# Two token tiles of values and gates placed ahead of the second half's recurrent units in a two-layer streaming encoder

## The chip, the cores and the metric

The program runs on one core of one Trainium2 chip. The metric is device microseconds of one execution. TensorE (PE) multiplies matrices into PSUM banks, VectorE (DVE) and ScalarE (ACT) do elementwise work and empty PSUM, GpSimd (POOL) does elementwise work on on-chip memory, and SyncE's queue (SP) issues most transfers.

## What is computed

One inference step for 576 tokens (64 sample tokens, then 512 prompt tokens) through two layers. Each layer is an FFN, a mixer and a second FFN, each between RMS norms. The mixer projects the normed input h once; the columns of that projection feed three head groups:

```python
h = _rmsnorm(x, ng[2])
z = h @ p['w_in'][l]
q_a, kv_a, kpe_raw, hq, hf, hi, hg, cu, cv = jnp.split(z, offsets, axis=-1)
o_a, c_new, kpe_new = _mla(q_a, kv_a, kpe_raw, pos, ...)
o_b, S_new = _hgrn2(hq, hf, hi, hg, lb_all[l], p['hgrn_out_g'][l], ...)
o_c, v_new = _chunk_mlp(cu, cv, p['cmlp_v_g'][l], p['cmlp_w_s'][l], p['cmlp_b_s'][l])
mix = jnp.concatenate([o_a, o_b, o_c], axis=-1) @ p['w_out'][l]
x = x + _rmsnorm(mix, ng[3])
```

The recurrent group (`_hgrn2`) takes queries hq and forget gates hf (4 x 128 columns in all), the values hi and the output gates hg (256 columns each), and scans over the tokens:

```python
S_new = exp(b_last)[..., None] * S + einsum('bshe,bshd->bhed', kc * exp(b_last[:, None] - b), vc)
o = _rmsnorm(o_inter + o_intra, out_g) * silu(hg)
```

## The kernel before

All matmuls of the projections are in split precision: a float32 operand is kept as a high part and a low part (tiles `hh`, `hl` of h; `wh`, `wl` of the weights), and a product is three matmuls (`three`, L144; `nat3`, L590). A weight chunk of 128x1024 (`chunk`, L118; `cols`, L131) is one transfer into `wr`, one ACT copy to `wh` (L126) and one DVE subtraction to `wl` (L127). The pool of `wr` has 6 buffers, those of `wh` and `wl` 7 each.

The 576 tokens are handled with features on the partitions in two halves of 288 columns (`HALF`). For tiles with tokens on the partitions there are five starts (`tcol`): columns 0, 64, 192, 320 and 448. A tile reads 128 columns from its start, so tiles 0 and 1 end at column 192, within the first half, and tile 2 reaches into the second.

The end of the FFN hands over half by half. For each half the generator `post` (L243) scales the eight feature tiles `d`, adds them into `x` and calls `pre` (L186), which makes `hh`, `hl` and the sum of squares (on POOL, L198). `pre_stats` (L200) then makes the factor of the norm: column sums on PE (`ss`, L68), a power on POOL (L151), a transposing spread on PE (`bc`, L73) and a copy to `rbc` on ACT (L215). The generators are stepped by an estimate of PE's time (`tick`, `until`). At the end of `units` for half 0, `zout(z, o, 0)` steps them until the first half's factor is there, and by their due times the whole `post` of the second half has then been issued.

In `mixer` (L1041) the four recurrent units `chs` (hq and hf, 128 columns each, chunks loaded ahead by the FFN) are multiplied for half 0 and then for half 1 (`units`, `together`, 8 k times 4 units times 3 matmuls, tile `u`). Each unit and half takes a PSUM bank of the tag "mm", which has 6. `zout` (L1035) evacuates the four banks of a half to `z` on DVE and scales them with `rbc`. Then `nat_chunks` asks for the four chunks `nch` of the 512 columns of values and gates (two k each), and `natural` (L597) multiplies them tile by tile (24 matmuls of 128x512 into one bank, tile `n`); ACT evacuates to `vg` with the factor `r` (L1066). After the first of the five, z of half 1 is evacuated and the generator `hgrn` (L645) is spawned. It makes `lf` and `k` (ACT, two table loads), a scan, and then 14 levels of DVE, ACT, POOL and PE work (`zb` L706, `lv`, `at` L721), beside which the main loop goes on with five tiles `uv` and five tiles of latents. It waits for all five `vg` only after the levels.

The order written out is a priority. The tile scheduler orders each engine's instructions by it and by when they are ready in its own estimate, and gives out buffers and banks as they come free; on the chip each engine then keeps that order. A buffer comes free with the last instruction that uses it.

Of the kernel before, what the change touches and what calls it, by code (L numbers as in the profile page):

```python
# [11 lines left out]
AF = mybir.ActivationFunctionType  # L12
# [24 lines left out]
RC = (0, 1, 3, 4, 5)  # L37
# [12 lines left out]
class Net:  # L50
# [990 lines left out]
    def mixer(self, l, gpost, gpre, nxt, packed):  # L1041
        nc, tin = self.nc, self.i
        w = tin["w_in"][l]
        r, r2 = self.rn, self.rn2
        c, a = {}, {"q": [], "qr": [], "kt": {}, "ktc": {}, "v": [], "vc": [], "oT": {}}
        self.mixh, self.mixl = {}, {}
        chs = self.ahead
        z = [self.slot("z") for _ in range(4)]
        for hf in (0, 1):
            o = self.units(chs, hf)  # L1050
            if hf == 0:
                self.zout(z, o, 0)
        self.stow()
        vg = {}
        self.left, self.attn_left, self.gated, self.decayed = 10, 20, False, False

        c["og"] = self.gain_rows("hgrn_out_g", l)
        nch = self.nat_chunks(w, 1216, 512)
        for i in range(5):
            ps = self.natural(nch, i, 512)  # L1060
            if i == 0:
                self.zout(z, o, 1)
                self.spawn(self.hgrn(l, z[2:], z[:2], vg))
                z = o = None
            t = self.slot("vg")
            nc.scalar.activation(t[:, :512], ps, AF.Copy, scale=r[:, RC[i]:RC[i] + 1])  # L1066
            vg[i] = t

        self.spawn(self.spatial(l, c))
        uv = []  # L1070
# [1 line left out]
        nch = self.nat_chunks(w, 1728, 512)  # L1072
        for i in range(5):
            ps = self.natural(nch, i, 512)
            t = self.slot("uv")
# [7 lines left out]
        nch = self.nat_chunks(w, 384, 320)  # L1083
# [3 lines left out]
        for i in range(5):  # L1087
            ps = self.natural(nch, i, 320)
# [6 lines left out]
        for u in range(3):  # L1095
            ps = self.unit(self.cols(w, u * P))
# [26 lines left out]
        def query(u):  # L1123
            ps = [self.mm("q"), self.mm("q")]
            for k in range(3):
                for (c0, n), pp in zip(HALF, ps):
                    self.three(pp[:, :n], wqh[k][:, u], wql[k][:, u], qah[k][:, c0:c0 + n], qal[k][:, c0:c0 + n], k == 0, k == 2)
                self.tick()
            return ps
# [47 lines left out]
        for h in range(HEADS):  # L1177
            ps = query(h)
# [8 lines left out]
            for c0, n in HALF:  # L1187
                ps = self.mm("k")
# [4 lines left out]
            ps = self.mm("k")  # L1193
# [14 lines left out]
        for k0 in (4, 0):  # L1208
# [5 lines left out]
            chs = {}  # L1214
# [242 lines left out]
```

## Time and profile before

| | |
|---|---|
| median of 3 runs | 2313.14 us (2313.03 to 2313.42) |
| the profiled execution | 2313.43 us |
| its span, first to last instruction | 2311.6 us |
| mean granted TensorE clock | 0.979 |
| PE busy | 2217.3 us (96%) |
| DVE busy | 1594.7 us (69%) |
| ACT busy | 1114.0 us (48%) |
| POOL busy | 225.4 us (10%) |

Busy shares are over the whole span; a stage can have another limit. PE's matmuls are pipelined and a shown duration overlaps the next; the spacing of starts gives the rate. Times in the views are microseconds from the span's start. Layer 0's change of stage is at about 412 to 465 us, layer 1's 1143.2 us later.

### The profile page before, as it was taken

The numbers are of one execution on the slowest core, as the hardware profiler recorded it, in microseconds if no ns is written. First come the engines' busy times: TensorE is split into PE (matmuls) and PEld (weight loads), VectorE is DVE, ScalarE is ACT, GpSimd is POOL, SyncE is SP. The second block draws the span as 40 slices with busy tenths as digits, with TensorE's granted clock in tenths as the row PEclk, the third lists the DMA queues.
The fourth block names the chain that finished last, engine by engine and source line by source line (L and its number), as shares of the span: only waits on it lengthen the run. The fifth ranks groups of instructions, "written<-read, shape, count | busy, mean of one in ns | idle before, by whom it ended". The sixth has DMA issues, their size and how long they took to land.

```text
span 2311.6 us, 39493 instructions
## 1 busy us (share of the span) xinstructions
PE 2217.3 (96%) x15892; PEld 2155.0 (93%) x15892; DVE 1594.7 (69%) x2671; ACT 1114.0 (48%) x1945; POOL 225.4 (10%) x230
## 2 busy tenths in 40 slices
PE   8999999998899899999989999999988998999998
PEld 7999999888799799999979999998887998999998
DVE  6888643787567888744588885438875678877443
ACT  7444442465554644443355444325646546444423
POOL 0000000343301100000020000004332020000000
PEclk9999999999999899999999999999999999999999
DMA  6333442222122233344123334423121312333421
GB/s 195 103 101 92 119 133 83 92 57 77 60 59 65 90 101 96 88 128 132 47 86 101 93 90 122 132 74 101 39 86 48 96 60 83 93 92 103 118 77 42
DMA packets 339787, 211.06 MB, mean 91 GB/s; under 512 B 17634, under 2 KB 319956, under 8 KB 339604
## 3 DMA queue, kind: packets, MB, share of 16 engines
q1 hardware_dynamic: 339604, 208.54, 30.3%
q8 instruction: 125, 2.05, 0.4%
q14 instruction: 58, 0.48, 0.1%
HBM read 190.11 MB, written 18.38 MB: 90 GB/s over the span
## 4 chain that ended last, share of the span: by engine, by line
PE 76%; DVE 14%; ACT 4%; issue 3%; POOL 3%; DMA 0%; SPq 0%; POOLq 0%; DVEq 0%; ACTq 0%
PE d L68 23%; PE X L68 22%; PE Q L68 11%; PE R L68 6%; PE wo L68 4%; PE u L68 3%; DVE zb L706 2%; PE n L68 2%; DVE hl L142 2%; DVE x L256 1%; PE sc L68 1%; DVE d L253 1%; DVE wl L127 1%; DVE wl L139 1%; PE q L68 1%
## 5 line engine op out<-in xcount | busy, mean ns | idle before, releaser
L68 PE MATMUL d<-gh,wh 128*128 128x288 f32 x1408 | 413.5, 297 | 2.7 <-ACT gh L138 2.7
L68 PE MATMUL d<-gl,wh 128*128 128x288 f32 x1408 | 413.9, 295 | 0.0
L68 PE MATMUL d<-gh,wl 128*128 128x288 f32 x1408 | 412.7, 294 | 0.0
L127 DVE TENSOR_TENSOR wl<-wr,wh 128x1024 fp32r<-128x1024 f32 (+2 forms) x174 | 203.4, 1173 | 175.9 <-ACT wh L126 175.1
L126 ACT ACTIVATE wh<-wr 128x1024 fp32r<-128x1024 f32 (+2 forms) x174 | 174.8, 1008 | 287.3 <-PE d L68 163.9
L68 PE MATMUL X<-th,wh 128*128 128x288 f32 x960 | 286.8, 299 | 0.0
L68 PE MATMUL X<-tl,wh 128*128 128x288 f32 x960 | 285.5, 297 | 0.0
L68 PE MATMUL X<-th,wl 128*128 128x288 f32 x960 | 284.5, 296 | 0.0
L68 PEld LDWEIGHTS d<-gh,wh 128*128 128x128 f32 x1408 | 262.3, 187 | 3.6 <-ACT gh L138 3.6
L68 PEld LDWEIGHTS d<-gh,wl 128*128 128x128 f32 x1408 | 264.8, 188 | 0.0
L68 PEld LDWEIGHTS d<-gl,wh 128*128 128x128 f32 x1408 | 264.1, 188 | 0.0
L138 ACT ACTIVATE wh<-wr 128x1024 fp32r<-128x1024 f32 x160 | 168.4, 1055 | 148.0 <-PE R L68 68.5
L139 DVE TENSOR_TENSOR wl<-ws,wh 128x1024 fp32r<-128x1024 f32 x120 | 147.0, 1225 | 105.4 <-ACT wh L138 105.2
L139 DVE TENSOR_TENSOR wl<-wr,wh 128x1024 fp32r<-128x1024 f32 x160 | 194.7, 1222 | 8.2 <-ACT wh L138 6.8
L138 ACT ACTIVATE wh<-ws 128x1024 fp32r<-128x1024 f32 x120 | 127.3, 1060 | 150.4 <-DVE ws L497 97.8
L151 POOL TENSOR_TENSOR p<-m,mhalf 128x3 f32<-128x3 f32 (+1 forms) x14 | 14.4, 1028 | 1739.4 <-DVE m L234 1535.1
L68 PEld LDWEIGHTS X<-th,wl 128*128 128x128 f32 x960 | 183.1, 191 | 0.0
L68 PEld LDWEIGHTS X<-tl,wh 128*128 128x128 f32 x960 | 182.8, 190 | 0.0
L68 PEld LDWEIGHTS X<-th,wh 128*128 128x128 f32 x960 | 182.6, 190 | 0.0
L390 DVE TENSOR_TENSOR d<-d,d 128x288 f32<-128x288 f32 x128 | 55.2, 454 | 179.6 <-PE d L68 179.5
L68 PE MATMUL u<-hh,wh 128*128 128x288 f32 x480 | 148.3, 312 | 3.0 <-ACT x L1363 1.5
L68 PE MATMUL u<-hl,wh 128*128 128x288 f32 x480 | 148.0, 309 | 1.2 <-DVE hl L142 1.2
(364 smaller groups left out, 5857.6 us busy)
## 6 DMA issues: line engine op xcount, KB each, us to landing
wr<-ffn_w_gate SPq DMA_DIRECT2D x160, 256.0 KB, 3.0
wr<-ffn_w_up SPq DMA_DIRECT2D x160, 256.0 KB, 3.4
wr<-ffn_w_down SPq DMA_DIRECT2D x64, 512.0 KB, 4.2
wr<-w_in SPq DMA_DIRECT2D x30, 512.0 KB, 3.7
xd<-x SPq DMA_DIRECT2D x48, 288.0 KB, 2.1
x<-xd SPq DMA_DIRECT2D x48, 288.0 KB, 6.0
wr<-ffn_w_down SPq DMA_DIRECT2D x32, 384.0 KB, 3.6
wr<-w_out SPq DMA_DIRECT2D x16, 512.0 KB, 3.4
```

The costliest lines, as they stand in the source:

```text
L68: self.nc.tensor.matmul(out, lhsT, rhs, start=start, stop=stop, skip_group_check=onto)
L126: nc.scalar.activation(hi[:, :a * b], raw[:, :a * b], AF.Copy)
L127: nc.vector.tensor_tensor(lo[:, :a * b], raw[:, :a * b], hi[:, :a * b].bitcast(F32), op=ALU.subtract)
L138: nc.scalar.activation(hi, src, AF.Copy)
L139: nc.vector.tensor_tensor(lo, src, hi.bitcast(F32), op=ALU.subtract)
L142: nc.vector.scalar_tensor_tensor(lo, src, scale, hi.bitcast(F32), op0=ALU.mult, op1=ALU.subtract)
L151: self.nc.gpsimd.tensor_tensor(out, m, self.mhalf[:, :n], op=ALU.pow)
L253: nc.vector.scalar_tensor_tensor(d[s][:, sl], d[s][:, sl], gpost[s], bc, op0=ALU.mult, op1=ALU.mult)
L256: nc.vector.tensor_tensor(self.x[k][:, sl], self.x[k][:, sl], d[k][:, sl], op=ALU.add)
L390: nc.vector.tensor_tensor(d[m][:, sl], d[m][:, sl], ps[hf][:, :n], op=ALU.add)
L706: nc.vector.tensor_tensor(zo, qv[rs, :, h:], ev[rs, :, h:], op=ALU.mult)
```

## The change

In `mixer` the loop over the halves is opened up. Between `zout(z, o, 0)` and the units of half 1, the chunks `nch` are asked for and `natural` runs for tiles 0 and 1, each with its ACT evacuation to `vg`. Then come the units of half 1, the stores of `x` (`stow`), the gains, `zout(z, o, 1)` directly, the spawn of `hgrn`, and tiles 2 to 4. The set of instructions is the same.

```diff
-        for hf in (0, 1):
-            o = self.units(chs, hf)
-            if hf == 0:
-                self.zout(z, o, 0)
+        vg = {}
+
+        def rows(nch, i):
+            t = self.slot("vg")
+            nc.scalar.activation(t[:, :512], self.natural(nch, i, 512), AF.Copy, scale=r[:, RC[i]:RC[i] + 1])
+            vg[i] = t
+
+        o = self.units(chs, 0)
+        self.zout(z, o, 0)
+
+        nch = self.nat_chunks(w, 1216, 512)
+        for i in range(2):
+            rows(nch, i)
+        o = self.units(chs, 1)
         self.stow()
-        vg = {}
         self.left, self.attn_left, self.gated, self.decayed = 10, 20, False, False
-
         c["og"] = self.gain_rows("hgrn_out_g", l)
-        nch = self.nat_chunks(w, 1216, 512)
-        for i in range(5):
-            ps = self.natural(nch, i, 512)
-            if i == 0:
-                self.zout(z, o, 1)
-                self.spawn(self.hgrn(l, z[2:], z[:2], vg))
-                z = o = None
-            t = self.slot("vg")
-            nc.scalar.activation(t[:, :512], ps, AF.Copy, scale=r[:, RC[i]:RC[i] + 1])
-            vg[i] = t
+        self.zout(z, o, 1)
+        self.spawn(self.hgrn(l, z[2:], z[:2], vg))
+        z = o = None
+        for i in range(2, 5):
+            rows(nch, i)
```

## Rows read from the trace of the kernel before

**Rows 1.** The page: busy us, share and count; then the chain's shares.

```profile
PE 2217.3 (96%) x15892; PEld 2155.0 (93%) x15892; DVE 1594.7 (69%) x2671; ACT 1114.0 (48%) x1945; POOL 225.4 (10%) x230
...
PE 76%; DVE 14%; ACT 4%; issue 3%; POOL 3%; DMA 0%; SPq 0%; POOLq 0%; DVEq 0%; ACTq 0%
```

**Rows 2.** The chain in order of time: start, duration, what, matmuls.

```profile
64.94 3.20 PE Q L68 x24
...
448.15 9.62 PE u L68 x60
...
458.79 14.77 PE n L68 x65
```

**Rows 3.** Windows: stretch, length, busy us (instructions) per engine, clock, DMA.

```profile
436.00:448.00 12.00, 7.99 (x59) 7.45 (x59) 11.45 (x23) 4.62 (x12) 6.92 (x7) 1.00 0.48 171
1579.20:1591.20 12.00, 9.42 (x59) 8.83 (x58) 11.45 (x23) 4.62 (x12) 6.95 (x7) 0.86 0.49 169
448.00:464.00 16.00, 16.00 (x92) 14.89 (x92) 7.71 (x12) 4.62 (x6) 4.03 (x10) 0.89 0.45 130
464.00:474.00 10.00, 10.00 (x50) 8.36 (x48) 6.57 (x8) 7.14 (x10) 3.77 (x3) 1.00 0.20 56
530.00:546.00 16.00, 11.52 (x75) 10.75 (x76) 15.01 (x25) 10.26 (x15) 4.86 (x4) 0.95 0.38 118
613.00:630.00 17.00, 14.38 (x56) 11.90 (x57) 7.04 (x21) 12.81 (x30) 1.83 (x3) 0.71 0.05 10
```

**Rows 4.** Timeline of PE: start, duration, instruction, idle before it and releaser.

```profile
442.19 0.63 PE L73 MATMUL bc<-ident_c,rn 64*128 64x64 f32 x3 [2.05 <-POOL rn L151]
...
447.32 0.83 PE L68 MATMUL ss<-ones,acc 128*128 128x1 f32 x6 [1.96 <-POOL acc L198]
...
449.05 0.44 PE L68 MATMUL u<-hh,wh 128*128 128x288 f32 x1
449.29 0.44 PE L68 MATMUL u<-hl,wh 128*128 128x288 f32 x1
...
457.61 0.39 PE L68 MATMUL n<-wh,hh 128*128 128x512 f32 x1
...
545.10 0.69 PE L73 MATMUL tp<-ident_c,cn 128*128 128x128 f32 x2 [4.48 <-DVE cn L897]
```

**Rows 5.** Timeline of DVE, layer 0: the splits of weights, z, the first lf.

```profile
429.75 1.21 DVE L127 TENSOR_TENSOR wl<-wr,wh 128x1024 fp32r<-128x1024 f32 x1
...
444.44 1.21 DVE L127 TENSOR_TENSOR wl<-wr,wh 128x1024 fp32r<-128x1024 f32 x1
...
446.54 1.54 DVE L1039 TENSOR_TENSOR z<-u,rbc 128x288 f32<-128x288 f32 x4
...
448.26 1.22 DVE L127 TENSOR_TENSOR wl<-wr,wh 128x1024 fp32r<-128x1024 f32 x1
...
457.97 2.36 DVE L127 TENSOR_TENSOR wl<-wr,wh 128x1024 fp32r<-128x1024 f32 x2 [5.89 <-ACT wh L126]
460.25 1.54 DVE L1039 TENSOR_TENSOR z<-u,rbc 128x288 f32<-128x288 f32 x4
...
467.43 1.22 DVE L668 TENSOR_SCALAR lf<-lf 128x576 f32<-128x576 f32 x1 [4.50 <-ACT lf L663]
```

**Rows 6.** Timeline of ACT, layer 0: a late chunk, then the start of hgrn.

```profile
449.77 1.06 ACT L126 ACTIVATE wh<-wr 128x1024 fp32r<-128x1024 f32 x1 [4.48 <-PE u L68]
...
463.69 0.69 ACT L1066 ACTIVATE vg<-n,rn 128x512 f32<-128x512 f32 x1 [3.56 <-PE n L68]
...
464.84 1.28 ACT L661 ACT_TABLE_LOAD   x1
466.14 0.69 ACT L661 ACTIVATE k<-z 128x576 f32<-128x576 f32 x1
```

**Rows 7.** Timeline of DVE, layer 1: chunk 1 of nch and z.

```profile
1587.64 1.21 DVE L127 TENSOR_TENSOR wl<-wr,wh 128x1024 fp32r<-128x1024 f32 x1
1589.76 1.54 DVE L1039 TENSOR_TENSOR z<-u,rbc 128x288 f32<-128x288 f32 x4
```

## The prediction

> **What bounds the kernel now.** I read the page first: TensorE (PE) is busy 96% of the span and carries 76% of the chain that ended last [rows 1], so mostly what counts is PE time. But the change touches one place per layer, so I went on to the windows there. From 436 to 448 us in layer 0, and from 1579.2 to 1591.2 us in layer 1, VectorE (DVE) is busy 11.45 of 12 us and PE only 7.99 and 9.42 [rows 3]. The reader is to see a stretch that PE doesn't bound: the norm of the second token half (`post`, `pre`) runs on DVE, ScalarE (ACT) and GpSimd (POOL) while PE has the recurrent units to do. Then the PE timeline for what ends PE's waits: 2.05 us for the factor of the first half (POOL, then `bc`), 1.96 us for POOL's sum of squares (`ss`) [rows 4]. That is 4.0 us per layer, the most that filler work could win there. Then the DVE and ACT timelines, for when the filler could start and what depends on its place [rows 5, 6], and the windows up to the end of the level loop of `hgrn`. From 530 to 546 us DVE is at 15.01 of 16 us, and PE stalls again, 4.48 us, for a DVE result [rows 3, 4]. So behind this place it is DVE, with `hgrn`'s chain, that sets the pace at least as much as PE.
>
> **What moves.** No instruction is added or removed. Per layer 48 matmuls of 128x512 (`natural` 0 and 1, 8 k times 3 each) and two ACT evacuations go ahead of the second half's 96 matmuls, and the 4 chunks of `nch` are now asked for before `units(chs, 1)`. A moved n matmul takes 14.77/65 = 0.227 us [rows 2]. A u matmul is 128x288, like the Q matmuls, which take 3.20/24 = 0.133 us [rows 2]. So 48 x 0.227 = 10.9 us of PE work per layer change place. Three resources decide when it really runs.
>
> *PSUM.* The tag "mm" has 6 banks. `units(chs, 0)` holds 4 until `zout(z, o, 0)`, which DVE does at 446.54 us [rows 5]. In the kernel before, the other two go to the first two units of half 1: of their 96 matmuls about 36 are done before the `ss` at 447.3 us, and 60 follow it [rows 2]. In the kernel after, natural 0 and 1 come earlier in the program and take these two banks, so none of the 96 can start before about 447 us. The filler displaces 36 x 0.133 = 4.8 us of work that already fills this hole.
>
> The Trainium skill ("Perfetto Trace Analysis", Identifying Performance Opportunities) says that a gap on the engine that should be busy can mean too little PSUM for the next tile. The trace is in line with it: 60 of the 96 run only after the evacuations of z have freed banks.
>
> *The weights of the filler.* A natural tile needs chunk 0 for k 0 and 1, chunk 1 for k 2 and 3, and so on. DVE finishes the low part of chunk 0 at 430.96 us, of chunk 1 at 445.65, of chunk 2 at 449.48 [rows 5]. Everything of `post` for both halves stands ahead of these splits in the program both before and after, so I leave these times where they are. Before 448 us, then, the filler has k 0 to 3 of two tiles: 24 x 0.227 = 5.4 us, against the 4.8 us displaced. That is 0.6 us won, not 4.0.
>
> *The seventh buffer.* The pool of high parts has 7 buffers; the recurrent chunks hold 4. So chunk 3 of `nch` is only split when the units let one go: ACT takes it at 449.77 us, after waiting 4.48 us for PE's u [rows 6]. In the kernel after, all four units end together, so chunk 3 and the chunks of the second `nch` come only then, and k 6 and 7 of both tiles (12 matmuls, 2.7 us) fall behind the units.
>
> **The sum, layer 0.** PE's u matmuls ahead of `ss` end at 447.32 - 1.96 = 445.4 us; the 36 of half 1 among them and the wait and `bc` (2.05 + 0.4, since the next start follows 0.4 us on) take 7.3, so the first half's units end at about 438. PE after: 12 n to 440.7, nothing until chunk 1 at 445.65, 12 n to 448.4, `ss` to 449.0, then 96 u and the 12 n of chunk 2: 12.8 + 2.7 = 15.5, to 464.5 us. Before, the units ended at 457.6 [rows 4], and at 464.5 PE had done (464.5 - 458.0)/0.227 = 29 of the n matmuls; after, it has done 36. PE would be 7 x 0.227 = 1.6 us ahead.
>
> Against that the clock: behind the two waits of before, u matmuls start 0.24 us apart instead of 0.133 [rows 4]; the mean granted clock from 448 to 464 us is 0.89 [rows 3], so part of it ran at the lower of the two levels (1.2 GHz, of 2.4). Some 13 matmuls are hit, 1.4 us lost. The new order leaves PE idle for 1.5 + 2.9 us with 0.6 us of `bc` between, so I expect the same fall, perhaps longer, meeting n matmuls also: between 0 and 3 us more lost than before. PE is then 1.6 us ahead to 1.4 us behind, so even.
>
> `hgrn` pays. Its z of half 1 was evacuated at 460.25 [rows 5], and moves to 464.5, or to 466.5 with the clock low: 4.2 to 6.2 us later. Some of that was slack: before, ACT held the first sigmoid until 466.14, because the evacuation of natural 0 (463.69) and a table load (464.84, 1.28) stood ahead [rows 6]. After, natural 0 ends later than the z, so the sigmoid only has chunk 3's split (1.06, the same instruction as at 449.77) and the table load ahead: 464.5 + 1.06 + 1.28 = 466.8 to 468.8, so 0.7 to 2.7 us late. On DVE, chunk 3's low part and two of the second `nch` (2.36 us at 457.97) were done before z; now they lie behind it. DVE then idles 4.50 us ahead of its first `lf` [rows 5], which hides one of them (1.2 us); the other two, 2.4 us, fall among instructions of a stretch in which DVE has 3.4 of 10 us free [rows 3]. Between 0 and 2.4 us; I take 1.3, as the free time is mostly waits inside the chain. Sum: 0.7 to 5.1 us late per layer, with 3.0 the middle (1.7 + 1.3). If that cover in the idle 4.50 us is gone, 1.2 more.
>
> Passed on to the end? The chain runs through `hgrn`'s DVE and ACT steps to 545 us, where PE waits 4.48 us for DVE [rows 4], so I pass it whole. Layer 1 has the same order (chunk 1 at 1587.64, z at 1589.76, as 444.44 and 446.54 moved by 1143.2) [rows 5, 7]; its clock fell earlier, in the window that shows 0.86 [rows 3]. Two layers: 2 x 3.0 = 6.0. The profiled execution took 2313.43 (span 2311.6), 0.3 above the median 2313.14; the forecast is 2313.1 + 6 = 2319, its own range 2314.5 (2 x 0.7) to 2323.3 (2 x 5.1).
>
> **Rivals.** *It washes out* (0.30). For: PE comes out even; the stretch from 613 to 630 us has PE busy 14.38 of 17 at a mean clock of 0.71 [rows 3], so a late `hgrn` may meet a wait that is there anyway; the sigmoid may move ahead of natural 0's evacuation and give back up to 4.3 us (466.14 less 461.79, the end of z). Also here: the tile scheduler, which orders by readiness, leaves the two banks with the units, and the change does nothing. Time 2311 to 2316, likeliest 2313.4.
>
> *It does what such an order is for* (0.20). If DVE splits chunks 1 and 2 before the last steps of `post`, 36 n matmuls (8.2 us) are ready, the 4.0 us of waits are filled, and the units still start at 447 us, so the 36 u displaced come back as 36 n that needn't run later: 4.0 us per layer, 2313.1 - 8 = 2305. Against: DVE has only 0.55 us free in that window [rows 3], and two splits are 2.4 us. It decides for this case if chunk 1's low part ends before about 441 us.
>
> By the Trainium skill ("Perfetto Trace Analysis", Optimization Strategy) interleaving regimes that load different engines can help; that speaks for this rival, and the DVE windows against it.
>
> *Worse than forecast* (within the forecast's chance): `ss` stands ahead of the second 12 n in PE's order, so these wait until 448 us, and the clock falls for longer: 2.5 us more per layer, 2324.
>
> **How the numbers follow.** Forecast 0.50, washed out 0.30, faster 0.20; the worse order is within the 0.50. About 0.2%, 4.6 us, is what a measurement here can tell from no change. The forecast case spans that bound (2 x 0.7 = 1.4 us at its low end), so I put 0.13 of its 0.50 under it, and 0.02 of the washed-out 0.30 above it. So faster 0.20, same 0.13 + 0.28 = 0.41, slower 0.37 + 0.02 = 0.39. The range for 8 in 10 runs from the faster rival's time, 2305, to the high end of forecast and worse order together, 2 x (5.1 + 2.5) = 15.2 above the median: 2328.
>
> **What would show it.** Right: between 438 and 447 us PE shows n matmuls and no u of half 1, with waits of over 2 us; 96 u after `zout`; z of half 1 evacuated at 464 to 467; the third and fourth n of each tile's chunks behind 445. Wrong: u of half 1 ahead of 446 us (the banks stayed); chunk 1's low part on DVE well before 444; first sigmoid at or before 466; the levels (`zb`, L706) ending where they did, though z is late, which would say that PE and not `hgrn` sets the end.

## The result and the profile after

| | before | after |
|---|---|---|
| median | 2313.09 us | 2336.83 us (2334.19 to 2339.29, 4 runs) |
| ratio to before, 95% interval | | 1.0104 [1.0087, 1.0122] |
| profiled execution, its span | 2313.43, 2311.6 us | 2335.09, 2333.3 us |

The kernel became slower by 23.7 us, or 12.0 us per layer by the ratio. The forecast was 2319 (2305 to 2328): the sign was right, and the time lies beyond the range.

The page of the kernel after (busy us, share, count; then the chain's shares), which answers to [rows 1]:

```profile
PE 2228.8 (96%) x15892; PEld 2160.4 (93%) x15892; DVE 1589.0 (68%) x2671; ACT 1113.9 (48%) x1945; POOL 225.0 (10%) x230
...
PE 77%; DVE 13%; ACT 3%; issue 3%; POOL 3%; DMA 0%; SPq 0%; POOLq 0%; DVEq 0%; ACTq 0%
```

The counts are the same, and no share moves by more than a point. The page alone would show nothing; the windows do. After (stretch, length, busy us with instructions of PE, PEld, DVE, ACT, POOL, clock, DMA share, GB/s), at the places of the first three of [rows 3], set to the later start of the stage (in layer 0 the first u starts at 422.37 us, where before has 421.50):

```profile
437.00:449.00 12.00, 6.41 (x34) 5.05 (x33) 11.45 (x23) 4.57 (x11) 6.93 (x7) 0.89 0.47 169
449.00:465.00 16.00, 16.00 (x91) 14.64 (x92) 1.32 (x3) 0.41 (x1) 0.86 (x1) 0.87 0.15 46
1590.60:1602.60 12.00, 7.54 (x34) 5.75 (x34) 11.45 (x24) 4.57 (x11) 6.92 (x7) 0.75 0.47 165
```

In the hole (the 12 us around PE's two waits) of layer 0 PE does 6.41 us of work where it did 7.99, in layer 1 7.54 for 9.42. In the 16 us behind it DVE has 1.32 us to do where it had 7.71, and ACT 0.41 for 4.62: the two engines that carry `hgrn`'s chain stand still while PE does the units. The timeline of PE, after (start, duration, instruction, idle before it and releaser), for [rows 4]:

```profile
438.45 0.30 PE L68 MATMUL u<-hh,wl 128*128 128x288 f32 x1
438.58 0.39 PE L68 MATMUL n<-wh,hh 128*128 128x512 f32 x1
...
443.06 0.63 PE L73 MATMUL bc<-ident_c,rn 64*128 64x64 f32 x3 [2.03 <-POOL rn L151]
443.45 0.48 PE L68 MATMUL n<-wh,hh 128*128 128x512 f32 x1
...
448.20 1.44 PE L68 MATMUL ss<-ones,acc 128*128 128x1 f32 x6 [3.57 <-POOL acc L198]
449.50 0.77 PE L68 MATMUL n<-wl,hh 128*128 128x512 f32 x1
...
450.92 0.63 PE L68 MATMUL n<-wl,hh 128*128 128x512 f32 x1
451.35 0.63 PE L68 MATMUL n<-wh,hl 128*128 128x512 f32 x1
...
454.03 0.30 PE L68 MATMUL u<-hh,wh 128*128 128x288 f32 x1
...
469.98 0.30 PE L68 MATMUL u<-hh,wl 128*128 128x288 f32 x1
```

Ten n stand ahead of `bc` and four ahead of `ss`; no u of the second half runs before 454.03. The wait for POOL's `acc` grew from 1.96 to 3.57 us, and the n behind it start 0.43 us apart instead of 0.227. DVE, after, for [rows 5]:

```profile
445.32 1.21 DVE L127 TENSOR_TENSOR wl<-wr,wh 128x1024 fp32r<-128x1024 f32 x1
...
447.42 1.54 DVE L1039 TENSOR_TENSOR z<-u,rbc 128x288 f32<-128x288 f32 x4
...
468.50 1.19 DVE L1039 TENSOR_TENSOR z<-u,rbc 128x288 f32<-128x288 f32 x3 [17.21 <-PE u L68]
469.61 1.22 DVE L127 TENSOR_TENSOR wl<-wr,wh 128x1024 fp32r<-128x1024 f32 x1
470.74 0.45 DVE L1039 TENSOR_TENSOR z<-u,rbc 128x288 f32<-128x288 f32 x1
471.11 3.49 DVE L127 TENSOR_TENSOR wl<-wr,wh 128x1024 fp32r<-128x1024 f32 x3
477.49 0.96 DVE L668 TENSOR_SCALAR lf<-lf 128x576 f32<-128x576 f32 x1 [2.89 <-ACT lf L663]
```

DVE idles 17.21 us for the units. The last z starts at 470.74; before, the one group of four began at 460.25. ACT, after, for [rows 6]:

```profile
468.30 3.90 ACT L126 ACTIVATE wh<-wr 128x1024 fp32r<-128x1024 f32 x4 [7.85 <-PE u L68]
472.66 0.69 ACT L1053 ACTIVATE vg<-n,rn 128x512 f32<-128x512 f32 x1 [0.46 <-PE n L68]
473.38 0.42 ACT L881 ACTIVATE vg<-vg 128x256 f32<-128x256 f32 x1
473.74 0.69 ACT L1053 ACTIVATE vg<-n,rn 128x512 f32<-128x512 f32 x1
474.46 0.42 ACT L881 ACTIVATE vg<-vg 128x256 f32<-128x256 f32 x1
474.90 1.28 ACT L661 ACT_TABLE_LOAD   x1
476.19 0.69 ACT L661 ACTIVATE k<-z 128x576 f32<-128x576 f32 x1
```

From the moment the units let buffers go, four chunk copies, two evacuations with their gates and a table load, 7.9 us, stand in ACT's queue ahead of the first sigmoid. It comes at 476.19 instead of 466.14.

The next views are of DVE's waits inside the 14 levels (engine, line, what it waited for: us in total, times, longest). Before, from 476.8 us:

```profile
DVE zb L706 <- ACT e L698: 5.8, 6, 1.3
```

After, from 488.7 us:

```profile
DVE zb L706 <- ACT e L698: 6.3, 4, 2.1
DVE at L721 <- PE lv L68: 4.9, 4, 1.9
DVE rk L895 <- POOL rk L151: 1.3, 2, 0.7
```

A wait is new: DVE comes to the masked copy `at` before PE has made its `lv`, four times, 4.9 us. The levels take 70.8 us from first to last `zb`, where they took 62.6.

### The profile page after: what moved, and what is told of

The parts are those of the page before. It is cut to its first block, busy times and chain, and to the rows that moved or that the text cites. A ratio compares the mean times of both kernels' runs of the same rounds, so it can differ in the third digit from the quotient of the medians.

```text
span 2333.3 us, 39500 instructions
## 1 busy us (share of the span) xinstructions
PE 2228.8 (96%) x15892; PEld 2160.4 (93%) x15892; DVE 1589.0 (68%) x2671; ACT 1113.9 (48%) x1945; POOL 225.0 (10%) x230
## 4 chain that ended last, share of the span: by engine, by line
PE 77%; DVE 13%; ACT 3%; issue 3%; POOL 3%; DMA 0%; SPq 0%; POOLq 0%; DVEq 0%; ACTq 0%
PE d L68 23%; PE X L68 22%; PE Q L68 10%; PE R L68 5%; PE wo L68 4%; PE n L68 3%; PE u L68 3%; DVE hl L142 2%; DVE zb L706 1%; DVE x L256 1%; PE sc L68 1%; DVE d L253 1%; DVE wl L127 1%; DVE wl L139 1%; POOL gr L151 1%
```

## The experiments

All times below count from the first u of the layer, which removes what earlier stages shift. "z" is the start of the last z of the second half, "k" the first sigmoid, "levels" the length from first to last `zb`, "lv" the last matmul of the levels, "n" the last `n<-wh,hh` (the last k) of the five-tile streams, "wo" the first matmul of the projection that ends the mixer; layer 0, in us. "Per layer" is the ratio less one, times 2313.1, over two.

| kernel | us | ratio, 95% | per layer | z | k | levels | lv | n | wo |
|---|---|---|---|---|---|---|---|---|---|
| before | 2313.1 | | | 39.8 | 44.6 | 62.6 | 129.6 | 138.5 | 239.4 |
| after | 2336.8 | 1.0104 [1.0087, 1.0122] | +12.0 | 48.4 | 53.8 | 70.8 | 141.6 | 145.2 | 251.4 |
| one tile ahead | 2321.7 | 1.0039 [1.0024, 1.0054] | +4.5 | 40.7 | 45.1 | 68.2 | 132.0 | 140.9 | 246.4 |
| none ahead | 2314.2 | 1.0007 [0.9997, 1.0016] | +0.8 | 38.3 | 38.4 | 64.9 | 118.3 | 138.0 | 240.0 |
| evacuations late | 2334.1 | 1.0093 [1.0078, 1.0108] | +10.8 | 48.4 | 48.4 | 73.8 | 136.8 | 141.0 | 247.2 |
| two units first | 2319.8 | 1.0033 [1.0021, 1.0046] | +3.8 | 45.4 | 41.4 | 73.0 | 132.4 | 136.0 | 242.9 |
| z and spawn late | 2324.0 | 1.0045 [1.0029, 1.0061] | +5.2 | 38.3 | 48.5 | 71.3 | 135.0 | 138.6 | 243.0 |
| k 0, 1 ahead | 2328.9 | 1.0066 [1.0049, 1.0082] | +7.6 | 46.6 | 47.7 | 67.1 | 128.2 | 147.3 | 249.8 |
| denser hgrn | 2345.3 | 1.0139 [1.0124, 1.0154] | +16.1 | 48.8 | 54.2 | 67.8 | 136.0 | 151.2 | 256.7 |
| forget first | 2302.3 | 0.9953 [0.9938, 0.9968] | -5.4 | 34.5 | 33.1 | 63.1 | 113.6 | 131.8 | 233.5 |
| banks held | 2332.1 | 1.0079 [1.0063, 1.0096] | +9.1 | 46.7 | 51.9 | 62.6 | 135.6 | 144.6 | 245.4 |
| banks held, later | 2328.1 | 1.0068 [1.0053, 1.0083] | +7.9 | 45.2 | 50.4 | 62.6 | 134.8 | 143.7 | 246.1 |
| spawn late | 2318.9 | 1.0028 [1.0017, 1.0039] | +3.2 | 38.0 | 48.1 | 70.4 | 133.7 | 137.3 | 242.8 |

### How much comes with the number of tiles

One tile ahead (against after: one tile in the first loop, four in the second), and none (no tile ahead, but `nch` early, and z and the spawn ahead of all five):

```diff
-        for i in range(2):
+        for i in range(1):
             rows(nch, i)
...
-        for i in range(2, 5):
+        for i in range(1, 5):
```

> Only tile 0 runs ahead of the second half's units, tile 1 goes back behind them. Theory A (late z): matmuls of the tiles that stand between the two z evacuations delay z of half 1 and with it hgrn, and each us of it reaches the end. One tile holds one bank and puts 18 to 24 n matmuls (4.1 to 5.4 us) ahead of z, so about half the loss: 2322 to 2326. Theory B (idle PE and low clock in the gap are the loss): the gap is as empty as with two tiles, so the loss stays mostly: 2330 to 2336. Theory C (the earlier request of the chunks and the new place of zout and hgrn are the loss): 2333 to 2337.

> No tile runs ahead; the chunks are still asked for before the second half's units, and zout and the spawn of hgrn still stand before all five tiles. Theory A: z of half 1 is back at its old time, and the first sigmoid no longer stands behind the evacuation of tile 0 (463.69 to 466.14 in the kernel before), so the time is that of before or up to 4.3 us per layer less: 2305 to 2313. Theory B: 2313. Theory C: the loss stays, 2330 to 2337.

One tile costs 4.5 us per layer, two cost 12.0, none 0.8, with an interval that includes zero. The first time is 0.3 us under theory A's range, the second about 1 us above A's and B's. So the early `nch` and the direct `zout` are not the cause. The kernel with none says more: its sigmoid is 6.2 us earlier than before, its last `lv` 11.2 and its last `zb` 2.0 us earlier, yet n and wo stay. An earlier `hgrn` alone brings nothing here: the stream of tiles on PE ends when it did.

### The late sigmoid

Against after, the evacuations of tiles 0 and 1 are written behind `hgrn`'s first step:

```diff
...
-        for i in range(2):
-            rows(nch, i)
+        held = [self.natural(nch, i, 512) for i in range(2)]
...
         self.spawn(self.hgrn(l, z[2:], z[:2], vg))
+        self.step(self.bg[-1])
+        for i in range(2):
+            put(i, held[i])
```

> The changed kernel, but the ACT evacuations of tiles 0 and 1 are written after hgrn's first step, so that ACT's order has the sigmoids ahead of them. Theory A: the sigmoid starts about 5 us earlier than in the changed kernel (it stood at 476.2 with both z ready at 471.2); if each us reaches the end, 2 x 5 less: 2326 to 2328. Theory B or C: the start of hgrn isn't the loss, 2334 to 2338.

The sigmoid came 5.4 us earlier, as the edit wants, and the time fell by 2.7 us in all, which the spread of the runs doesn't tell from nothing (the two intervals overlap); 9 to 11 were expected. So the queue on ACT in front of the sigmoid, the most striking rows of after, is not what most of the 23.7 us hang on.

### The banks

Against after, two of the four units of the second half are put ahead of the two tiles, so that they get the two free banks, and the other two behind:

```diff
+        o = self.units(chs[:2], 1)
         for i in range(2):
             rows(nch, i)
-        o = self.units(chs, 1)
+        o += self.units(chs[2:], 1)
```

> Two of the four units of half 1 first, then tiles 0 and 1, then the other two units; everything else as changed. The two free banks go to units again and PE's gap is filled as before the change. Theory A: 36 to 48 n matmuls (8 to 11 us) still stand ahead of the last z, so most of the loss stays: 2327 to 2334. A variant of B (the banks: PE's hole left empty is the loss): 2313 to 2318.

All 48 n still run ahead of the last u, but the hole is filled by u, as this window shows against [rows 3]:

```profile
439.50:451.50 12.00, 9.94 (x63) 9.62 (x62) 11.45 (x22) 5.13 (x12) 6.26 (x7) 0.86 0.43 148
```

PE has 9.94 us of work there, and the cost falls from 12.0 to 3.8 us per layer; the time lies between the two ranges written down, nearer to the banks'. This points to the two banks and not to the work put ahead of the units. It doesn't settle it, since the forget units are evacuated early here too and the sigmoid comes 12.4 us earlier than in after; the kernels with the banks held do. Next, the reverse: the tiles take the banks, but only the 12 n whose weights are ready (k 0 and 1 of both tiles) are written ahead.

```diff
...
-        for i in range(2):
-            rows(nch, i)
+        begun = [self.natural(nch, i, 512, None, range(2)) for i in range(2)]
...
+        for i in range(2):
+            rows(nch, i, begun[i], range(2, KT))
```

> Both tiles take their banks ahead of the units, but only k 0 and 1 (12 matmuls) are written ahead; the other 36 come behind z and hgrn's first step. The banks are taken and PE's gap is as empty as in the changed kernel; what is gone is the work between the two z evacuations. If the hole alone costs (2.4 to 4.5 us per layer by the traces): 2318 to 2322. If the banks and the hole were the whole loss of 12 us per layer: 2333 to 2337. If only the displaced work cost: 2311 to 2315.

With 18 n ahead of the last u, where after has 38, 7.6 us per layer remain; the time, 2328.9, is in none of the ranges written down, and nearest to that of the whole loss. Last, the order of before, with the two banks held by empty tiles until z of the first half is out. The first version (held from before the first half's units) also took banks from those, which then needed 20.5 us from first to last start instead of 16.1; the second asks for the banks only behind them. Each adds two memsets and two copies of one column per layer. In the second these don't delay the hole: `bc` and `ss` start 20.7 and 25.5 us after the first u, in before 20.7 and 25.8.

```diff
             if hf == 0:
+                hold = [self.mm("hold") for _ in range(2)]
+                for t in hold:
+                    nc.vector.memset(t[:, 0:1], 0.0)
                 self.zout(z, o, 0)
+                for t in hold:
+                    nc.vector.tensor_copy(t[:, 0:1], z[3][:, 0:1])
+                hold = None
```

> The kernel before in its own order, with the two free banks held by an empty tile each until z of half 0 is evacuated (four instructions of one column on DVE more per layer). No tile of values moves. It prices the banks alone: none of the second half's 96 matmuls can run in the hole. Hole theory: 36 x 0.133 = 4.8 us of PE work leaves the hole, z of half 1 is 5 to 6 us late, and with the low clock 4.5 to 7 us per layer are lost: 2322 to 2327. If instead the order of the tiles is the loss and the banks are not: 2313 to 2315.

> The order of the kernel before, but in each layer the two free banks of the tag mm are held by empty tiles that are asked for once the first half's units have been issued, and let go when z of the first half has been evacuated. So the first half's units should keep their banks (ending about 16.5 us after their start, as before) and only the second half's 36 early u matmuls lose theirs; no n matmul fills the gap. Theory (two costs that add: the gap open, and hgrn begun with fewer tiles of values behind it): the gap's share alone, 4.5 to 6 us per layer, 2322 to 2325. Rival (the lost banks cost only what the displaced matmuls take where they ran, 36 x 0.133 = 4.8 us, part of it won back by clock and by the waits that were there anyway): 2314 to 2320. Rival (the banks are nearly the whole cost of the changed kernel): 2329 to 2336.

PE of the second version:

```profile
438.78 0.29 PE L68 MATMUL u<-hh,wl 128*128 128x288 f32 x1
443.44 0.63 PE L73 MATMUL bc<-ident_c,rn 64*128 64x64 f32 x3 [4.37 <-POOL rn L151]
448.20 1.44 PE L68 MATMUL ss<-ones,acc 128*128 128x1 f32 x6 [4.13 <-POOL acc L198]
449.50 0.59 PE L68 MATMUL u<-hh,wh 128*128 128x288 f32 x1
449.89 0.44 PE L68 MATMUL u<-hl,wh 128*128 128x288 f32 x1
```

and its row of the chain (start, duration, what, matmuls), which stands where [rows 2] has the 60 u:

```profile
449.64 15.08 PE u L68 x96
```

With nothing else changed, all 96 u run behind `ss`. The waits are 8.50 us instead of 4.01. The levels have before's length to 0.1 us, and z, lv, n and wo are all later by 5.2 to 6.6 us: nearly a rigid shift. The Trainium skill ("Perfetto Trace Analysis", Optimization Strategy) says that the same gap, repeated over a stretch, can mean too little SBUF or PSUM for the next tile. This case points the same way: two banks fewer, and PE idles twice as long. This hole alone costs 7.9 us per layer [6.1, 9.6] by the ratio, 6.2 in the profiled executions. That is more than the 4.5 to 6 that I expected and more than the 4.8 us of work displaced; the time, 2328.1, lies between that range and the one for banks that are nearly the whole cost, and nearer to the second. The first version, 2332.1, is above its range too. The runs don't split the excess cleanly: 4.5 us are the longer waits, about 0.6 the longer stretch at the lower clock, and the rest is behind z.

### The place of `hgrn`

In before, z of the second half and the spawn are moved behind the second tile; then the spawn alone:

```diff
-            if i == 0:
+            if i == 1:
                 self.zout(z, o, 1)
                 self.spawn(self.hgrn(l, z[2:], z[:2], vg))
```

> The kernel before, with z of half 1 evacuated and hgrn spawned behind tile 1 instead of tile 0; no bank, no chunk and nothing in PE's gap changes. It prices a late hgrn alone. Theory A (each us of a late hgrn reaches the end): the sigmoid moves behind a second evacuation and silu, 5 to 6 us later, 2 x 5 more: 2322 to 2325. Theory P (what counts is PE's lost time in the gap and where PE waits; hgrn's start has slack, as the earlier sigmoid of the run with late evacuations gave back only 1.3 us per layer): 2313 to 2318.

```diff
             if i == 0:
                 self.zout(z, o, 1)
+            if i == 1:
                 self.spawn(self.hgrn(l, z[2:], z[:2], vg))
```

> The order of the kernel before, but hgrn is spawned behind the second tile of values instead of the first; z of the second half is still evacuated behind the first. This takes apart the late kernel's +5.3 us per layer (z and spawn both one tile later). If the late z is what costs: time near before, 2313 to 2316. If the place of the spawn, and with it the order in which ACT and DVE take hgrn's first steps against chunks and evacuations, is what costs: 2321 to 2325, with the first sigmoid at about 48 us after the first u and the levels stretched to about 70 us.

Both give the same milestones: z no later than in before (38, where before has 39.8), the sigmoid at 48, levels of 70 to 71 us. So it is the place of the spawn that does it; writing z behind the second tile too adds some 2 us per layer, not clear of noise, as the two intervals overlap. The first, 2324.0, is where theory A had it. The time with the spawn alone late, 2318.85, lies between the two times written down. DVE's waits inside the levels with the spawn late, from 482.2 us:

```profile
DVE at L721 <- PE lv L68: 6.9, 5, 2.0
DVE zb L706 <- ACT e L698: 5.2, 4, 2.1
DVE rk L895 <- POOL rk L151: 1.3, 2, 0.7
```

and of PE in the same stretch:

```profile
PE lv L68 <- DVE zb L706: 4.8, 3, 1.8
PE tp L73 <- DVE cn L897: 0.9, 1, 0.9
```

PE waits for DVE's `zb`, and DVE for PE's `lv`, each in its turn. Before had 1.0 us of the first wait and none of the second; after has both (2.9 and 4.9 us). What else stands between the first and the last `zb` has changed too: eight weight splits for six, and the latents' `rk` and `cn`, which in before come behind the last `zb`. With fewer tiles of values behind the spawn, the streams that follow reach into the levels. The kernels bear this out: with three tiles behind the spawn, 8 or 9 DVE instructions of the latents lie between the first and the last `zb` and the levels take 70 to 74 us (denser hgrn apart); with four or more there is none, and they take 63 to 68. The waits in turn are not what the long levels share: with two units first DVE waits 0.1 us for `lv`, and the levels still take 73.0. How the 8 us divide among these was not tried apart.

Denser steps of `hgrn` (after, with its pace of 3.0 us set to 2.5):

```diff
-        self.pace, self.apace, self.l1, self.l2, self.l3 = 3.0, 2.16, 1.26, 3.94, 2.15
+        self.pace, self.apace, self.l1, self.l2, self.l3 = 2.5, 2.16, 1.26, 3.94, 2.15
```

> The changed kernel with the pace of hgrn's levels in the planner set from 3.0 to 2.5, so that the 14 levels are written 7 us earlier against the main loop. Theory O (the levels fall behind since hgrn is spawned with three instead of four tiles of values left, and they stretch from 62.6 to 70.8 us): part comes back, 2325 to 2332. Theories A and P: the start and the hole are the loss, 2334 to 2340.

The last `lv` comes 5.5 us earlier than in after and the tiles end 6.0 later, and the whole is 8.4 us slower, above both ranges written down. Hurrying the chain doesn't pay here: inside the levels PE now waits 9.3 us for `zb`, where it waited 2.9 in after.

### A better order

If the banks belong to the units and the chain wants an early start, the two forget units, which `hgrn` reads first, should be multiplied and evacuated first; no tile runs ahead. The edit, against after:

```diff
-    def zout(self, z, o, hf):
+    def zout(self, z, o, hf, us=range(4)):
...
-        for u in range(4):
+        for u in us:
...
-        for i in range(2):
-            rows(nch, i)
-        o = self.units(chs, 1)
+        o = self.units(chs[:2], 1)
+        self.zout(z, o, 1, (0, 1))
+        o += self.units(chs[2:], 1)
...
-        self.zout(z, o, 1)
+        self.zout(z, o, 1, (2, 3))
         self.spawn(self.hgrn(l, z[2:], z[:2], vg))
...
-        for i in range(2, 5):
+        for i in range(5):
             rows(nch, i)
```

> No tile ahead; of half 1 the two forget units are multiplied and evacuated before the other two, so that hgrn's sigmoids can start some 8 us earlier than in the kernel before, while PE does the query units. Theory A: 2 x 5 to 2 x 8 less, 2297 to 2304. Theory P: PE sets the end of the stretch, 2310 to 2316.

It is faster than both kernels, and within the range of theory A: 2302.30 us, ratio 0.9953 [0.9938, 0.9968]. PE and ACT:

```profile
442.94 0.63 PE L73 MATMUL bc<-ident_c,rn 64*128 64x64 f32 x3 [2.04 <-POOL rn L151]
...
449.06 0.72 PE L68 MATMUL ss<-ones,acc 128*128 128x1 f32 x6
```

```profile
448.72 2.01 ACT L126 ACTIVATE wh<-wr 128x1024 fp32r<-128x1024 f32 x2 [2.69 <-PE u L68]
453.66 0.41 ACT L215 ACTIVATE rbc<-bc 128x288 f32<-128x288 f32 x1 [2.93 <-PE bc L73]
454.09 1.28 ACT L661 ACT_TABLE_LOAD   x1
455.38 0.69 ACT L661 ACTIVATE k<-z 128x576 f32<-128x576 f32 x1
```

The second wait is gone: all 48 u of the two forget units lie in the hole, where before had 36 of the second half's, and `ss` comes with no idle time before it. The sigmoid is 11.5 us earlier than in before. Here n ends 6.8 us earlier too, which an early sigmoid alone didn't bring. PE's waits from the first u to the last n add up to 5.6 us, where before has 11.1: the 1.96 at `ss`, 1.0 inside the levels, and 2.4 of those behind them are gone.

## Why the prediction was wrong

**What held.** The sign, though I had given a slower kernel only 0.39. The mechanism of the banks: no u of the second half ran before `zout`, and 36 u were displaced. The low part of chunk 1 at 445.32, where I left it, which ended the rival with the faster time by its own condition (before 441). The last chunks split only when the units let go. And that a late chain is passed on whole: with the banks held later, z is 5.3 us later and wo 6.6.

**PE's order in the hole: the first term that failed.** I had 24 n ahead of 448.4 and the first u at 449.0; there were 14, and the first u came at 454.03. `ss` stood ahead of the remaining 10, the order that I had called worse and priced at 2.5 us. With two n of chunk 2 they took 4.53 us (449.50 to 454.03) where 12 x 0.227 is 2.7: 2.7 for the place, 1.8 for the clock. The other 0.5 of the 5.0 is no loss, as the whole stage starts 0.87 us later in this execution. "PE even" fell with it: the units ended 11.6 us later than before counted from the first u, not 6.9. I had put the clock's share at 0 to 3 us for PE's total, but not into the time at which the units end, on which `hgrn` depends.

**The sigmoid.** The sum had it 0.7 to 2.7 us late, and it was 9.2 late (10.05 in the span's own times). z is 7.4 late by its first instruction and 8.5 by its last, since a split now runs between them; I had 4.2 to 6.2. I had counted on slack behind it: one chunk copy and a table load, 2.3 us, would have put the sigmoid at 473.5. But four copies, two evacuations and two gates stood ahead of it, as their places in the program are ahead of the spawn, and it came at 476.19. That the evacuation ends behind z was right, but it doesn't put it behind the sigmoid. The term for DVE's displaced splits, 1.3, was nothing: DVE still idled 2.89 us before `lf`, and the splits were done before that wait. These sizes matter less than they look: with the evacuations out of the way, 5.4 us of the sigmoid's lateness went, and with it some 1.3 us per layer of the time, not clear of noise.

**The term that was missing.** I moved `hgrn`'s chain as a block of fixed length. Its levels grew by 8.2 us in layer 0 and 9.9 in layer 1, with one tile fewer (three for four) between its start and the streams that follow. The late spawn, which has the hole filled, shows this place by itself, with a sigmoid 3.5 us later and levels 7.8 longer: 3.2 us per layer [2.0, 4.5]. The number of tiles is not all that sets the levels' length: with one tile ahead and with k 0, 1 ahead they grew by 5.6 and 4.5 us with four or more tiles behind the spawn, and why stays open.

**The sum as the runs have it.** The kernels make a table of two by two:

| us per layer | hole filled | hole opened by the lost banks |
|---|---|---|
| `hgrn` with four or five tiles behind it | 0 (before), 0.8 (none ahead) | 7.9 (banks held, later), 7.6 (k 0, 1 ahead) |
| with three | 3.8 (two units first), 3.2 (spawn late) | 12.0 (after) |

7.9 + 3.2 = 11.1, within after's interval of 10.1 to 14.1. (With the spawn late there are three whole tiles behind it, as in after.) The terms' own intervals, [6.1, 9.6] and [2.0, 4.5], are wide, so this agrees with two costs that add, and doesn't prove it. My 3.0 per layer was some 0.4 of the first term and nothing of the second. The wash-out that I gave 0.30 asked for slack in `hgrn` or on PE. The runs show none: an earlier chain alone wins nothing (none ahead), and a later one costs at once (spawn late). That fits a kernel before in which chain and stream of tiles end together, so that delay of either is paid; where the two meet was not traced.

## What to carry to other kernels

Filler put ahead of a stage takes more than time: ask which buffers or banks it gets, who had them, and whether its own operands are ready by then; here work that could run was displaced by work that could not. A chain that is started later among the streams beside it is not moved as a block: count which work falls between its steps at the new place. And where an earlier chain alone wins nothing, look for an order that brings the stream beside it forward too, as the one with the forget units first did.

## What the runs showed of the hardware

In these runs TensorE's clock falls to the lower of its two levels behind the gap, and filling the second wait doesn't spare it. With the banks held, the granted clock in the 4.70 us behind the two waits, and in the time that follows:

```profile
449.50:454.20 4.70, 4.70 (x20) 4.70 (x21) 1.96 (x7) 0.00 (x0) 4.13 (x10) 0.50 0.58 175
454.20:462.00 7.80, 7.80 (x59) 7.80 (x59) 0.00 (x0) 0.00 (x0) 0.08 (x1) 0.99 0.02 7
```

0.50 is 1.2 GHz. With the forget units first, PE waits only for `bc`, 2.04 us, and is then busy without a break; still the clock falls, 1.3 us after the wait has ended (442.94 to 444.24):

```profile
437.00:443.00 6.00, 3.96 (x30) 3.72 (x29) 5.46 (x12) 2.61 (x6) 3.36 (x5) 1.00 0.47 178
443.00:449.00 6.00, 6.00 (x34) 5.93 (x35) 6.00 (x12) 2.24 (x6) 4.49 (x5) 0.72 0.50 164
```

About 13 u run 0.24 us apart there, from 444.24 on, as many as in before behind both waits [rows 4]. So the clock costs some 1.4 us whether 36 or 48 u lie in the hole, and some 2.0 with none in it (banks held later, about 20 u at the lower level).

The 28 `zb` of the levels took 26.8 us in before, 23.6 in after and 21.4 with the spawn late, with the same shapes. In layer 0 they are of two sorts, at most 0.57 us or 0.85 to 1.69 us. Each of the 13 long ones in before starts while POOL is at a product `w` (L700) and ends about 0.3 us behind it. Here is one such pair in before; the DVE row is a long `zb` and a short one together:

```profile
496.98 1.56 POOL L700 TENSOR_TENSOR w<-k,e 128x576 f32<-128x576 f32 x1 [2.43 <-ACT e L698]
497.16 2.15 DVE L706 TENSOR_TENSOR zb<-z,e 64x288 f32<-64x288 f32 x2
```

After has 12 long ones and the spawn late 9, so the difference lies mainly in how many meet POOL's work. Why they do was not tried.
